# GLA level operands prepared two levels ahead, and background steps moved inside the seven-product units

## The chip, the cores and the metric

One NeuronCore of a Trainium2 chip runs the whole program in one launch. The metric is the device time of one execution in microseconds (us). Five engines matter: TensorE (PE) does matmuls, VectorE (DVE) and ScalarE (ACT) do elementwise work and empty the matmul banks (PSUM), GpSimd (POOL) does a little elementwise work and issues some transfers, and SyncE (SP) issues most of the transfers. Each engine works through its own instruction list in order.

## The reference

One decoder layer of width 1024 over 512 tokens, all in float32. After a layer norm, one input projection feeds gated linear attention (GLA, 4 heads), latent attention (MLA, 8 heads) and the gates; the two branches are gated and projected out; a second layer norm and a squared-ReLU MLP of hidden width 4096 follow.

```python
q_g, k_g, v_g, r_g, a_lr, q_lat, kv_lat, gate_logits = split(h @ w_in)
log_a = log_sigmoid(a_lr @ w_gla_a2 + b_gla_a2) / 16
o_gla = gla(q_g, k_g, v_g, log_a)            # o_t = q_t S_t, S_t = diag(a_t) S_{t-1} + k_t^T v_t
y_gla = (rms_norm(o_gla) * silu(r_g)) @ w_o_gla
y_mla = merge_heads(mla(q_lat, kv_lat)) @ w_o_mla
h = layer_norm(ALPHA * h + (g_gla * y_gla + g_mla * y_mla) @ w_out)
out = layer_norm(ALPHA * h + square(relu(h @ w_ff1)) @ w_ff2)
```

## The kernel before, in words

**Weights.** A weight strip of 512 KB is loaded into a buffer `wraw` (three buffers; SP queue, line 176). ACT copies its rounded part to `whi` (line 191), DVE the remainder to `wlo` (line 192), two buffers each. Every product is then three matmuls: high by high, and the two cross terms. Three places (the output-gate projection `proj_r`, the branch gates `g0` and `g1`, the first MLP matrix `f1`) use a scheme with seven block products instead of eight; in `proj_r` some summed weights and in `g0`/`g1` also the summed activations (`sh`) come from DRAM. The summed weights of a gate unit are made by loading one block into a buffer `wq` from SP (line 1181) and adding a second block to it by an accumulating transfer issued from POOL (line 1183).

**GLA by levels.** `gla_levels(h)` computes, for one head, the 512x512 causal score matrix by halving: for spans s = 1, 2, 4, ... 256 it fills the blocks in which a query and a key are in neighbouring spans of length s. The operand `qk` holds query and key of the head and is scaled in place from level to level. One level consists of

- `update(s)` (line 804, DVE): multiply `qk` in place by the decays of level s;
- `pack(2s)` (line 812, two ACT instructions; line 809 for s = 128): copy the rows that the next level needs into a buffer `M`;
- two matmuls on `M` into a bank `px` (line 864; line 867 for s = 128; line 871 takes s = 256 straight from `qk`);
- `take` (line 817, two DVE instructions): copy the wanted elements of that bank into the score buffer `SD`.

Because the scaling is in place, `pack(2s)` needs `update(s)`, and the next update needs `pack(2s)` to have read.

**What sets the order.** The program is written as one main sequence of matrix products, beside which background routines (Python generators) are stepped: `lane_levels` runs `gla_levels` for heads 0 to 3, `lane_out` the outputs `gla_out` of each head (lines 914 to 936), `r_out` the evictions of `proj_r`, `h_load` the loads of `sh`. `tick(n)` steps the first n routines once, `finish` and `levels_upto` step some until they end. A scheduler that simulates the program turns this into one fixed instruction list for each engine, so the places of the ticks and the order of the statements in a generator change the lists, and nothing is decided at run time. Main sequence around the change: values of heads 0 and 1 (`proj_v(0)`, lines 281 to 283), `proj_r` (lines 752 to 754), values of heads 2 and 3 (`proj_v(1)`, lines 247 to 283 are the general products), then the gate units `g0` and `g1` (lines 1208 to 1210), with the rest of the GLA in between.

**Names.** In the lists, `px_1914` or `M_1901` is one allocation; line numbers shift a little in the changed kernel: 804, 809, 812 and 817 become 803, 808, 811 and 816; 850 stays; 864 to 936 and 1181 to 1233 become higher by two; 1249 becomes 1250.

Of the kernel before, what the change touches and what calls it, by code (L numbers as in the profile page):

```python
# [52 lines left out]
def tile_hybrid_block(ctx: ExitStack, tc: tile.TileContext, I, out, dbg=None):  # L53
# [36 lines left out]
    def PX(shape=(P, T), dt=F32, n="px"):  # L90
        return px.tile(list(shape), dt, tag="px", name=nm(n))
# [132 lines left out]
    def tick(width):  # L224
        for g in list(active[:width or WID[0]]):
            step(g)
# [79 lines left out]
    PL["k"] = plan("w_in", C_K, T)  # L306
    WQ = {}

    RY, RA4 = (4, 4, 2, 2, 1, 2, 2), "t1"
    RW = (("11", 0), ("21", 1), ("t2", 3), ("t1", 2), ("t3", 6), ("22", 5), ("t4", 4))  # L310

    def r_src(op, hf):
# [394 lines left out]
    def proj_r():  # L707
        bank, e, xs = {}, {}, {}

        def x_load(ph):  # L710
            xs[ph] = []
            for p in range(4):
                t = B([P, 2, 256], F32R, "xr")
                x = (2, 3, 5, 6).index(ph)
                nc.sync.dma_start(f(t), hsd[p][x // 2][:, x % 2])
                xs[ph].append((t[:, 0], t[:, 1]))

        def r_out(ph, bank, e):
            for t in range(2):
                a, b = bank["a", t], bank["b", t]  # L720
                if ph == 4:
                    silu(0, 2 + t, a)
                else:
                    o, x, y, op, j, tt = {1: (0, b, e.get((0, t)), ALU.add, 0, t), 6: (2, e.get((2, t)), a, ALU.subtract, 1, 2 + t),
                                          5: (3, b, e.get((3, t)), ALU.subtract, 1, t)}[ph]
                    vtt(e[o, t], x, y, op=op)
                    yield
                    silu(j, tt, e[o, t])
                yield

        nat = {0: (0, 0), 1: (1, 0), 4: (1, 1)}
        for n, (op, ph) in enumerate(RW):
            if n + 1 < len(RW) and RW[n + 1][1] not in nat:
                x_load(RW[n + 1][1])
            if ph in nat:
                i, h = nat[ph]
                x = [tuple(hT[2 * p + i][:, w, 256 * h:256 * h + 256] for w in range(2)) for p in range(4)]
            else:
                x = xs.pop(ph)
            opens = ph in (0, 1, 2)  # L740
            for hf in range(2):
                it = PL["r"][2 * n + hf]
                pump(it)
                hi, lo = stream[it]["w"]
                for pp in range(2):
                    xh, xl = x[2 * hf + pp]
                    for t in range(2):
                        key = ("a" if ph in (0, 3, 6, 4) else "b", t)
                        if ph in (0, 1) and not hf and not pp:
                            bank[key] = MM()  # L750
                        o, c = bank[key], slice(t * P, (t + 1) * P)
                        mm(o, xh[:, c], hi[:, pp], start=opens and not hf and not pp, stop=False, skip_group_check=True)  # L752
                        mm(o, xh[:, c], lo[:, pp], start=False, stop=False, skip_group_check=True)
                        mm(o, xl[:, c], hi[:, pp], start=False, stop=hf == 1 and pp == 1, skip_group_check=True)
                    if (hf, pp) != (1, 1):
                        tick(None)
            if ph in (0, 3, 2):
                for t in range(2):
                    e[ph, t] = B([P, T], F32, "er")
                    act(e[ph, t], bank["b" if ph == 2 else "a", t], AF.Copy)  # L760
            else:
                spawn(r_out(ph, bank, e))
                if ph in (4,):
                    finish(active[-1])
            tick(None)

            if op == RA4:
                r_acc4()
# [22 lines left out]
    def gla_levels(h):  # L791
# [10 lines left out]
        def update(s):  # L802
            v = lr(qk, s)
            vtt(v, v, view(D, off[s] + 1, (2, T // (2 * s)), (-1, 2), (0, s)), op=ALU.mult)

        def pack(s):
            M = B([P, T], F32, "M")
            if s == 128:
                act(M.rearrange("p (n two s) -> p n two s", two=2, s=s), lr(qk, s), AF.Copy)
            else:  # L810
                for i, w in enumerate((T + 256 + s, T + s - 256)):
                    act(pairs(M[:, i * 256:(i + 1) * 256], s), view(k0, i * 256, (2 * s, 128 // s), (w, 2), (1, s)), AF.Copy)
            return M

# [26 lines left out]
        vtt(v, v, view(D, 1, (2, T // 2), (-1, 2)), op=ALU.mult)  # L841
        v = view(k0, T + 1, (2, T // 2))
        vtt(v, v, D[:, T:T + T // 2], op=ALU.mult)
        yield
        px1 = []
        for i in range(2):
# [2 lines left out]
                c = (2 * i + t) * P  # L849
                mm(p[:, t * 192:(t + 1) * 192], x0[:, c:c + P], xs[i][:, t, :], start=True, stop=True)  # L850
            px1.append(p)
        M = pack(2)
        yield
        for i, p in enumerate(px1):
            pt = p[:, :384].rearrange("p (t c) -> p t c", c=192)
# [3 lines left out]
        prev, s = None, 2  # L859
        while s < T:  # L860
            p = PX()
            if s <= 64:
                for i in range(2):
                    mm(p[:, i * P:(i + 1) * P], M[:, i * P:(i + 1) * P], M[:, 256 + i * P:256 + (i + 1) * P], start=True, stop=True)
            elif s == 128:
                for i in range(2):
                    mm(p[:, i * P:(i + 1) * P], M[:, 2 * i * P:(2 * i + 1) * P],
                       M[:, (2 * i + 1) * P:(2 * i + 2) * P], start=True, stop=True)
            else:
                for j in range(2):  # L870
                    mm(p[:, j * 256:(j + 1) * 256], qk[:, 0, j * P:(j + 1) * P], qk[:, 1, 256:], start=True, stop=True)
            if prev is not None:
                take(*prev)
            prev = (s, p)
            if s < 256:
                update(s)
            s *= 2
            if s < 256:
                M = pack(s)
            if s == 16 and h + 1 < GH:  # L880
                decays(h + 1)
            yield
# [302 lines left out]
    def unit(key, ops, evac, after=None, pb=None):  # L1185

        bank, e1, e5, u2 = {}, {}, {}, {}

        def prod(op):
            ph = dict(FMO)[op]  # L1190
            opens = ph in (0, 2, 1)
            for g in range(UNITS[key][2]):
                bk = ("a" if ph in (0, 3, 6, 4) else "b" if ph in (2, 5) else "c", g)
                if ph == 1 and key == "g0":
                    bank[bk] = bank["b", g]
                elif opens:
                    bank[bk] = (PX if ph == 1 else (pb or MM) if ph == 2 else MM)()
                o, it = bank[bk], PL[key, op, g]
                pump(it)
                hi, lo = stream[it]["w"]  # L1200
                for k in range(4):
                    while len(ops) <= k or ph not in ops[k]:
                        tick(3)
                    xh, xl = ops[k][ph]
                    for a in range(2):
                        c = slice(a * P, (a + 1) * P)
                        oa = o[:, a * 256:(a + 1) * 256]
                        mm(oa, hi[:, k, c], xh, start=opens and k == 0 and a == 0, stop=False, skip_group_check=True)  # L1208
                        mm(oa, hi[:, k, c], xl, start=False, stop=False, skip_group_check=True)  # L1209
                        mm(oa, lo[:, k, c], xh, start=False, stop=k == 3, skip_group_check=True)  # L1210
                    if k == 1:
                        tick(3)
                if ph == 0:
                    e1[g] = B([P, T], F32, "e1")
                    act(e1[g], o, AF.Copy)
                elif ph == 1:
                    vtt(e1[g], o, e1[g], op=ALU.add)
                    evac(0, 0, g, e1[g], True)
                elif ph == 2:
                    e5[g] = B([P, T], F32, "e5")  # L1220
                    act(e5[g], o, AF.Copy)
                elif ph == 3:
                    u2[g] = B([P, T], F32, "u2")
                    act(u2[g], o, AF.Copy)
                if ph == (5 if key == "g0" else 3):
                    vtt(u2[g], bank["b", g], u2[g], op=ALU.subtract)
                    evac(1, 0, g, u2[g], True)
                if ph == 6:
                    vtt(e5[g], e5[g], o, op=ALU.subtract)
                    evac(1, 1, g, e5[g], True)  # L1230
                elif ph == 4:
                    evac(0, 1, g, o, False)
                tick(3)
            if after:
                after(op)
        return prod
# [101 lines left out]
    t1, mv = mla_pair(1)  # L1338
# [345 lines left out]
```

## Time and profile before

| | |
|---|---|
| median of 3 executions | 882.56 us (882.06 to 883.23) |
| the profiled execution | 882.95 us |
| its span, first to last instruction | 881.1 us |
| PE busy, and its share of the span | 859.6 us, 98% |
| mean granted PE clock | 0.996 |
| DVE, ACT, POOL busy | 72%, 53%, 16% |

All times below are counted from the start of the span, and the 1.85 us between span and execution time lie outside it. A row of a timeline gives start, length, engine, source line, operation and tiles, then in brackets how long the engine was idle before it and what it had waited for. Matmuls overlap: a 128x256 matmul of 0.28 us is followed by the next after 0.12 us. A windows row gives, for a stretch of the span, the busy time of each engine with its instruction count, the granted PE clock (1.00 is full), the busy share of the 16 transfer engines (it passes 1 where packets overlap) and the rate.

### The profile page before, as it was taken

The page shows a single profiled execution, that of the slowest core. Times are in us where ns is not written, and L with a number is a line of the kernel's source. Part 1 is how long each engine was busy: PE and PEld are TensorE (multiplying, and loading weights), DVE is VectorE, ACT ScalarE, POOL GpSimd, SP SyncE. Part 2 cuts the span into 40 slices and gives each one's busy share as a digit, 9 for nine tenths or more (in the row PEclk, how much of TensorE's full clock was granted, in tenths as well). Part 3 has the DMA queues.
Part 4 walks back from the last instruction along what each step waited for, and adds up shares of the span by engine and source line. Part 5 has one row for each costly group of instructions (what it writes and reads, how often), then busy time and mean ns, then how long its engine had stood idle before and what let it go on. Part 6 is the DMA issues. An engine that isn't in the chain of part 4 may idle for free.

```text
span 881.1 us, 12813 instructions
## 1 busy us (share of the span) xinstructions
PE 859.6 (98%) x4765; PEld 750.3 (85%) x4765; DVE 634.4 (72%) x1037; ACT 469.0 (53%) x821; POOL 144.6 (16%) x184
## 2 busy tenths in 40 slices
PE   5999999999999999999999999999999999999996
PEld 5988888889989978888888888988888888889985
DVE  7959988877655646656766798886567646788865
ACT  5556767654565624435554414566357446656820
POOL 0323305030101030300000003004400520141000
PEclk9999999999999999999999999999999999999999
DMA  7995945595828443321207527007931990499312
GB/s 240 282 232 146 332 145 121 191 267 198 197 70 197 141 130 102 102 66 58 93 26 270 183 84 275 1 0 192 281 101 40 270 240 25 89 236 227 119 63 79
DMA packets 95213, 134.57 MB, mean 153 GB/s; under 512 B 12672, under 2 KB 58112, under 8 KB 95152
## 3 DMA queue, kind: packets, MB, share of 16 engines
q1 hardware_dynamic: 73840, 92.36, 33.3%
q0 software_dynamic: 19392, 37.76, 19.8%
q10 hardware_dynamic: 1920, 3.66, 1.1%
q8 instruction: 37, 0.61, 0.3%
q14 instruction: 24, 0.20, 0.1%
HBM read 110.15 MB, written 8.91 MB: 135 GB/s over the span
## 4 chain that ended last, share of the span: by engine, by line
PE 94%; DVE 2%; ACT 2%; DMA 1%; issue 0%; POOLq 0%; SPq 0%; DVEq 0%; ACTq 0%
PE mm L247 11%; PE mm L248 11%; PE mm L249 11%; PE mm L283 5%; PE mm L281 5%; PE mm L282 5%; PE mm L1208 4%; PE mm L1210 4%; PE mm L1209 4%; PE px L1496 2%; PE px L1495 2%; PE px L1497 2%; PE mm L1496 2%; PE mm L1495 2%; PE mm L1497 2%; PE mm L752 1%
## 5 line engine op out<-in xcount | busy, mean ns | idle before, releaser
L192 DVE TENSOR_TENSOR wlo<-wraw,whi 128x1024 fp32r<-128x1024 f32 (+1 forms) x90 | 99.3, 1104 | 92.1 <-ACT whi L191 85.7
L191 ACT ACTIVATE whi<-wraw 128x1024 fp32r<-128x1024 f32 (+1 forms) x90 | 85.6, 951 | 91.3 <-PE mm L248 43.4
L248 PE MATMUL mm<-h,whi 128*128 128x512 f32 x224 | 87.2, 389 | 0.0
L247 PE MATMUL mm<-h,whi 128*128 128x512 f32 x224 | 87.1, 390 | 0.0
L249 PE MATMUL mm<-h,wlo 128*128 128x512 f32 x224 | 83.2, 390 | 0.0
L192 DVE TENSOR_TENSOR wlo<-wq,whi 128x1024 fp32r<-128x1024 f32 x44 | 54.0, 1226 | 32.2 <-ACT whi L191 32.2
L1514 POOL DMA_DIRECT2D res<-ev x42 | 37.7, 1035 | 184.3 <-ACT ev L1512 150.5
L191 ACT ACTIVATE whi<-wq 128x1024 fp32r<-128x1024 f32 x44 | 46.5, 1058 | 34.7 <-PE mm L1209 22.2
L1210 PE MATMUL mm<-sh,wlo 128*128 128x256 f32 x176 | 50.0, 284 | 0.0
L1209 PE MATMUL mm<-sh,whi 128*128 128x256 f32 x176 | 49.8, 283 | 0.0
L1208 PE MATMUL mm<-sh,whi 128*128 128x256 f32 x176 | 49.8, 283 | 0.0
L249 PEld LDWEIGHTS mm<-h,wlo 128*128 128x128 f32 x224 | 42.0, 188 | 9.1 <-DVE wlo L192 0.4
L247 PEld LDWEIGHTS mm<-h,whi 128*128 128x128 f32 x224 | 42.1, 188 | 8.7
L248 PEld LDWEIGHTS mm<-h,whi 128*128 128x128 f32 x224 | 42.0, 188 | 8.7
L191 ACT ACTIVATE xh<-wraw 128x1024 fp32r<-128x1024 f32 (+1 forms) x28 | 27.2, 987 | 28.0 <-PE mm L283 15.6
L192 DVE TENSOR_TENSOR xl<-wraw,xh 128x1024 fp32r<-128x1024 f32 (+1 forms) x28 | 31.3, 1131 | 9.0 <-ACT xh L191 9.0
L1557 ACT ACTIVATE relu<-mm 128x512 f32<-128x512 f32 x24 | 14.1, 596 | 42.0 <-PE mm L249 42.0
L1208 PEld LDWEIGHTS mm<-sh,whi 128*128 128x128 f32 x176 | 33.8, 192 | 0.0
L1209 PEld LDWEIGHTS mm<-sh,whi 128*128 128x128 f32 x176 | 33.8, 192 | 0.0
L1210 PEld LDWEIGHTS mm<-sh,wlo 128*128 128x128 f32 x176 | 33.8, 192 | 0.0
L1208 PE MATMUL mm<-h,whi 128*128 128x256 f32 x112 | 31.9, 285 | 1.2 <-ACT whi L191 1.2
L1210 PE MATMUL mm<-h,wlo 128*128 128x256 f32 x112 | 32.0, 285 | 0.7 <-DVE wlo L192 0.7
(481 smaller groups left out, 2704.3 us busy)
## 6 DMA issues: line engine op xcount, KB each, us to landing
wraw<-in_w_ff_dram SPq DMA_DIRECT2D x36, 512.0 KB, 5.1
wraw<-in_w_in_dram SPq DMA_DIRECT2D x30, 512.0 KB, 4.5
wq<-in_w_ff_dram POOLq DMA_DIRECT2D x26, 512.0 KB, 8.9
res<-ev POOLq DMA_DIRECT2D x42, 256.0 KB, 9.8
wq<-in_w_in_dram SPq DMA_DIRECT2D x20, 512.0 KB, 6.3
wq<-in_w_in_dram POOLq DMA_DIRECT2D x18, 512.0 KB, 9.7
hsd<-hs SPq DMA_DIRECT2D x16, 256.0 KB, 4.4
xr<-hsd SPq DMA_DIRECT2D x16, 256.0 KB, 4.2
```

What stands on the lines that cost most here:

```text
L191: st["ins"] = act(hi[:, :nk, :n], raw[:, :nk, :n], AF.Copy)
L192: st["lo"] = vtt(lo[:, :nk, :n], raw[:, :nk, :n], f(hi[:, :nk, :n]), op=ALU.subtract)
L247: mm(o, hi[:, c], xh, start=first, stop=False)
L248: mm(o, hi[:, c], xl, start=False, stop=False)
L249: mm(o, lo[:, c], xh, start=False, stop=last)
L281: mm(o, xh, hi[:, :n], start=opens, stop=False, skip_group_check=share)
L282: mm(o, xh, lo[:, :n], start=False, stop=False, skip_group_check=share)
L283: mm(o, xl, hi[:, :n], start=False, stop=last, skip_group_check=share)
L1208: mm(oa, hi[:, k, c], xh, start=opens and k == 0 and a == 0, stop=False, skip_group_check=True)
L1209: mm(oa, hi[:, k, c], xl, start=False, stop=False, skip_group_check=True)
L1210: mm(oa, lo[:, k, c], xh, start=False, stop=k == 3, skip_group_check=True)
L1514: nc.gpsimd.dma_start(res[tt + t][:, j * T:(j + 1) * T], e, accum_op=ALU.add)
```

## The change

Three edits.

1. In `gla_levels`, the operands are made two levels ahead of their product. `pack(2)` comes before the first yield, `update(2)` and `pack(4)` right after the first products; in the loop, after the product of level s come `update(2s)` and `pack(4s)`, and only then `take` of the level before. The same operations are done, with one more `M` buffer alive.
2. In `proj_r`, the ticks move from behind a slice (both token halves) to between its two halves, at three of the four slices of a product; the tick after the eviction goes. That is 21 ticks for 28.
3. In `unit`, the two ticks of a product stand in its first and third slice, not in the second and after the eviction.

```diff
-    RY, RA4 = (4, 4, 2, 2, 1, 2, 2), "t1"
+    RY, RT, RA4 = (4, 4, 2, 2, 1, 2, 2), ((0, 0), (1, 0), (1, 1)), "t1"
...
                         mm(o, xl[:, c], hi[:, pp], start=False, stop=hf == 1 and pp == 1, skip_group_check=True)
-                    if (hf, pp) != (1, 1):
-                        tick(None)
+                        if t == 0 and (hf, pp) in RT:
+                            tick(None)
...
                 if ph in (4,):
                     finish(active[-1])
-            tick(None)
...
+        Ms = [pack(2)]
         yield
         px1 = []
...
             px1.append(p)
-        M = pack(2)
+        update(2)
+        Ms.append(pack(4))
         yield
...
             p = PX()
+            M = Ms.pop(0) if s < 256 else None
             if s <= 64:
...
+            if s <= 64:
+                update(2 * s)
+            if s <= 32:
+                Ms.append(pack(4 * s))
             if prev is not None:
                 take(*prev)
             prev = (s, p)
-            if s < 256:
-                update(s)
             s *= 2
-            if s < 256:
-                M = pack(s)
...
-                    if k == 1:
+                    if k % 2 == 0:
                         tick(3)
...
                 elif ph == 4:
                     evac(0, 1, g, o, False)
-                tick(3)
```

The number of instructions is the same on every engine (PE has 4685 matmuls in both). PE's list differs only from the values of heads 0 and 1 up to the end of the first gate products, apart from two neighbouring transposes that change places far later; the lists of the other engines differ in the same stretch. Three places show what moves.

**PE, last GLA head (head 3), in `proj_v(1)`.** `M` is the packed operand of a level, `px` the bank of its product; lines 914 to 916 (916 to 918 in the changed kernel) are output products of another head, lines 281 to 283 products of `proj_v(1)`. Before, the products of levels 4, 8 and 16:

```order
L283 MATMUL mm_2013<-whi_2005,h_21_140 128x512
L864 MATMUL px_1914<-M_1901 128x128 x2
L864 MATMUL px_1936<-M_1920 128x128 x2
L864 MATMUL px_1963<-M_1942 128x128 x2
L914 MATMUL px_1973<-vh_1341,sd_1367 128x256
L915 MATMUL px_1973<-vl_1342,sd_1367 128x256
L916 MATMUL px_1973<-vh_1341,sd_1367 128x256
L864 MATMUL px_2021<-M_1969 128x128 x2
L914 MATMUL px_2030<-vh_1341,s_281_1370 128x256
```

Now, the products of levels 2, 4 and 8 and what follows:

```order
L282 MATMUL mm_1961<-wlo_2008,h_27_156 128x512
L866 MATMUL px_2051<-M_1984 128x128 x2
L866 MATMUL px_2070<-M_2021 128x128 x2
L283 MATMUL mm_1961<-whi_2007,h_27_156 128x512
L866 MATMUL px_2100<-M_2055 128x128 x2
L936 MATMUL px_2109<-ca,og_2079 128x128 x2
L936 MATMUL px_2109<-ca,og_2080 128x128 x2
L281 MATMUL mm_1921<-whi_2090,h_30_164 128x512
```

Three level products of this head still stand close together. But between the head's first products (line 850) and its first level product lie 38 rows of other work now, where 2 rows lay between them before; and the later levels are spread over the following strips. In the same way head 1's last three products on `M` (lines 864, 864, 867), which stood in three consecutive rows of PE's list before, now have three 512-wide products of `proj_r` between each two.

**ACT, end of unit `g0`.** `whi` is the split of the next weight strip, `osq` squares of GLA outputs, `gt` gates, `u` an eviction; before, the strip `whi_2763` (last block, first half) is placed ahead of the eviction `u_2625`, and PE's list has that block's products ahead of those of block t3, second half (`whi_2729`):

```order
L191 ACTIVATE whi_2729<-wq_2000 128x1024
L918 ACTIVATE osq_2583,gss_2570<-px_2571 128x256
L191 ACTIVATE whi_2763<-wq_2431 128x1024
L918 ACTIVATE osq_2611,gss_2570<-px_2601 128x256
L1249 ACTIVATE gt_2673<-e_521_2479,hbg 128x256
L1249 ACTIVATE gt_2675<-e_521_2479,hbg 128x256
L1224 ACTIVATE u_544_2625<-mm_2361 128x512
```

Now:

```order
L191 ACTIVATE whi_2721<-wq_1912 128x1024
L920 ACTIVATE osq_2593,gss_2580<-px_2581 128x256
L920 ACTIVATE osq_2617,gss_2580<-px_2607 128x256
L1226 ACTIVATE u_544_2625<-mm_2353 128x512
L1250 ACTIVATE gt_2717<-u_544_2625,hbg 128x256
L1250 ACTIVATE gt_2719<-u_544_2625,hbg 128x256
L191 ACTIVATE whi_2763<-wq_2419 128x1024
L1250 ACTIVATE gt_2673<-e_521_2479,hbg 128x256
L1250 ACTIVATE gt_2675<-e_521_2479,hbg 128x256
L920 ACTIVATE osq_2649,gss_2580<-px_2607 128x256
L191 ACTIVATE whi_2796<-wq_2421 128x1024
```

The eviction `u` moved ahead of the next strip, and PE takes the blocks in the order in which they are written: t3 first half, t3 second half, then the last block's two halves.

**SP, loads for `proj_v(1)` and `g0`.** `wraw` are the strips of `proj_v(1)`, `wq` the blocks for `g0`. Before, the four strips stand ahead of the six blocks:

```order
L176 DMA wraw_1885<-in_w_in_dram 128x2x512
L176 DMA wraw_1924<-in_w_in_dram 128x2x512
L176 DMA wraw_2003<-in_w_in_dram 128x2x512
L176 DMA wraw_2080<-in_w_in_dram 128x2x512
L1181 DMA wq_1987<-in_w_in_dram 128x4x256
L1181 DMA wq_1990<-in_w_in_dram 128x4x256
L1181 DMA wq_1993<-in_w_in_dram 128x4x256
L1181 DMA wq_1995<-in_w_in_dram 128x4x256
L1181 DMA wq_1997<-in_w_in_dram 128x4x256
L1181 DMA wq_2000<-in_w_in_dram 128x4x256
```

Now:

```order
L176 DMA wraw_1832<-in_w_in_dram 128x2x512
L1183 DMA wq_1899<-in_w_in_dram 128x4x256
L1183 DMA wq_1902<-in_w_in_dram 128x4x256
L176 DMA wraw_1857<-in_w_in_dram 128x2x512
L1183 DMA wq_1905<-in_w_in_dram 128x4x256
L1183 DMA wq_1907<-in_w_in_dram 128x4x256
L1183 DMA wq_1909<-in_w_in_dram 128x4x256
L1183 DMA wq_1912<-in_w_in_dram 128x4x256
L176 DMA wraw_1915<-in_w_in_dram 128x2x512
L176 DMA wraw_2005<-in_w_in_dram 128x2x512
```

The second strip of `proj_v(1)` now stands behind two of `g0`'s blocks, the third and the fourth behind all six.

## The prediction

> **What bounds the kernel now.** The page comes first. Its chain, followed back from the last instruction, is almost all matmul work, so only time in which PE stands still, or runs slowly, is to be had:
>
> ```profile
> PE 94%; DVE 2%; ACT 2%; DMA 1%; issue 0%; POOLq 0%; SPq 0%; DVEq 0%; ACTq 0%
> ```
>
> Next the waits view for PE alone (total us, times, longest). Besides the start of the program, four kinds of wait matter, and all lie where the change moves instructions:
>
> ```profile
> PE px L864 <- ACT M L812: 2.0, 2, 1.0
> PE mm L1208 <- ACT whi L191: 1.2, 1, 1.2
> PE px L867 <- ACT M L809: 0.8, 1, 0.8
> PE mm L1210 <- DVE wlo L192: 0.7, 1, 0.7
> ```
>
> The windows view, cut at these waits, shows that nothing else between 97 and 300 us is idle: the four stretches below hold all of the missing 203.00 - 198.37 = 4.63 us. The second also has a lower clock.
>
> ```profile
> 143.00:146.00 3.00, 2.25 (x14) 1.84 (x14) 3.00 (x8) 2.72 (x6) 0.00 (x0) 1.00 0.91 248
> ...
> 181.00:189.00 8.00, 6.03 (x36) 5.58 (x35) 5.81 (x18) 3.23 (x10) 2.07 (x2) 0.79 1.17 256
> ...
> 246.00:249.00 3.00, 1.79 (x14) 1.51 (x13) 1.84 (x2) 2.60 (x8) 0.00 (x0) 1.00 0.00 0
> ...
> 256.00:258.00 2.00, 1.31 (x11) 1.10 (x10) 2.00 (x3) 1.97 (x4) 0.00 (x0) 1.00 0.00 0
> ...
> sum 203.00, PE 198.37 PEld 181.98 DVE 152.56 ACT 122.12 POOL 32.92; mean PE 22.04 PEld 20.22 DVE 16.95 ACT 13.57 POOL 3.66
> ```
>
> **What one wait costs.** It is more than its idle time: the row before it, otherwise overlapped by its follower, runs out alone, and the row after it is longer. PE's timeline at the longest wait:
>
> ```profile
> 246.26 0.28 PE L1209 MATMUL mm<-sh,whi 128*128 128x256 f32 x1
> 246.38 0.28 PE L1210 MATMUL mm<-sh,wlo 128*128 128x256 f32 x1
> 247.87 0.38 PE L1208 MATMUL mm<-h,whi 128*128 128x256 f32 x1 [1.21 <-ACT whi L191]
> 248.09 0.28 PE L1209 MATMUL mm<-h,whi 128*128 128x256 f32 x1
> ```
>
> The usual start-to-start is 0.12 us. Here 246.38 to 247.87 is 1.49, and 247.87 to 248.09 is 0.22: lost 1.37 + 0.10 = 1.47 us for 1.21 us of idle, so 0.26 us on top of each wait.
>
> **Term 1, head 1 at 144 us.** Three level products stand in a row on PE; the last needs a pack that ACT reaches late:
>
> ```profile
> 140.58 0.63 ACT L788 ACTIVATE dec<-gs 128x508 f32<-128x508 f32 x1 [1.30 <-POOL gs L786]
> ...
> 143.62 0.61 ACT L809 ACTIVATE M<-qk 128x512 f32<-128x512 f32 x1
> ```
>
> In the new ACT list this pack follows `dec` at once, since the level's update no longer waits for a product to be taken. So it is ready at about 141.2 + 0.6 = 141.8; counting PE's new list with the row spacings of before, the product comes at 142.9. Gain 0.75 + 0.26 = 1.0 us, margin about 1 us. The one `M` more that is alive I put at nothing: it comes from a pool of 22 buffers, whose return no row here is waiting for; if a pack had to wait for one, that would take the margin and cost up to one pack, 0.6 us.
>
> **Term 2, head 3 at 181 to 185 us.** PE's waits, and ACT's packs for the successive levels:
>
> ```profile
> 182.74 0.71 PE L864 MATMUL px<-M 128*128 128x128 f32 x4 [0.95 <-ACT M L812]
> ...
> 184.84 1.22 PE L864 MATMUL px<-M 128*128 128x128 f32 x4 [1.03 <-ACT M L812]
> ```
>
> ```profile
> 178.31 0.73 ACT L812 ACTIVATE M<-qk 128x256 f32<-128x256 f32 x2 [1.87 <-DVE qk L804]
> ...
> 180.15 0.73 ACT L812 ACTIVATE M<-qk 128x256 f32<-128x256 f32 x2 [0.58 <-DVE qk L804]
> 181.96 0.72 ACT L812 ACTIVATE M<-qk 128x256 f32<-128x256 f32 x2 [1.09 <-DVE qk L804]
> ...
> 184.07 0.72 ACT L812 ACTIVATE M<-qk 128x256 f32<-128x256 f32 x2
> ```
>
> A level comes each 1.81 to 2.11 us, and PE asks for several in a row. The change does not shorten the step from update to pack, for scaling in place keeps them serial; it starts the steps earlier relative to the products. Three packs now need about 2 x 1.84 + 0.73 = 4.4 us from the first, while PE has 38 rows, by my count 8.6 us, between the head's first products and its first product on `M`. Even with the two operands' splits in between, some 3 us are left. Gain 0.95 + 1.03 + 2 x 0.26 = 2.5 us. DVE is the queue on which the wait could return: the update stands behind og and split work there, and the packs, and behind them on ACT the next strip's split, would be late with it.
>
> **Term 3, the clock.** Right after these two waits:
>
> ```profile
> 184.90:188.30 3.40, 3.40 (x16) 0.51 1.18 238
> ```
>
> ```profile
> 181.40:184.80 3.40, 1.47 (x11) 1.06 (x9) 3.40 (x12) 2.84 (x8) 0.77 (x1) 1.00 1.16 266
> 244.60:248.00 3.40, 2.19 (x19) 1.98 (x18) 1.54 (x3) 1.60 (x5) 0.00 (x0) 1.00 0.00 0
> ```
>
> For 3.40 us PE ran at 0.51: 3.40 x 0.49 = 1.67 us lost. The 3.40 us before held 1.47 us of work, 43%; around the longest single wait 64% was left and no drop followed. I take it that a drop needs something between, so it goes with term 2.
>
> [...]
>
> **Term 4, the gate unit at 246 and 256 us.** ACT and then DVE:
>
> ```profile
> 246.40 0.39 ACT L918 ACTIVATE osq<-px 128x256 f32<-128x256 f32 x1 [2.36 <-PE px L916]
> ...
> 246.77 1.05 ACT L191 ACTIVATE whi<-wq 128x1024 fp32r<-128x1024 f32 x1
> ```
>
> ```profile
> 255.99 1.23 DVE L192 TENSOR_TENSOR wlo<-wq,whi 128x1024 fp32r<-128x1024 f32 x1
> ```
>
> At 246 the split of the last block waited behind an `osq` that needs PE; at 256 the `wlo` of its second half ended at 257.22, and PE went on at 257.27. PE's new list has the t3 blocks in their natural order: a strip's buffer is free when the first t3 product ends, 24 matmuls x 0.12 = 2.9 us before the next strip is needed, and the split takes 1.05 + 1.23 = 2.3 us. Gain 1.47 + 0.69 + 0.26 = 2.4 us, with a margin of only 0.6 us for the `wlo` of each strip.
>
> **The sum.** 1.0 + 2.5 + 1.67 + 2.4 = 7.6 us: 882.95 - 7.6 = 875.35 against the profiled execution, if nothing returns. Of the three tight places (head 1's pack, two `wlo`) I let two come back at the smallest size, 0.69 + 0.26 = 0.95 each: 877.25. The profiled run lies 0.39 us above the median, so 876.9. Bounds: none back gives 875.0; two back and the clock with them 878.5. The fewer ticks of `proj_r` cost no instruction; they could only make head 3 late, which is the next rival.
>
> **Rivals.**
>
> *A wait at head 3 stays.* Three of its products still stand almost in a row. If PE meets the chain there, two waits of today's size and the clock return, 2.5 + 1.67 = 4.2: 882.95 - 7.6 + 4.2 - 0.39 = 879.2. Against it: the 8.6 us of other work.
>
> *The waits only move* (the change does not do what it says). The step per level is unchanged, and elsewhere (head 0's products on `M` also stand three in a row now) as much could be lost as is won: 882.95 - 0.39 = 882.6, with 881 as its lower end. For it: 1.8 us per level on ACT and DVE. Against it: PE now has the longer stretches of work between levels.
>
> [...]
>
> *Slower: strips late behind `g0`'s blocks.* SP now issues all six blocks ahead of the third strip of `proj_v(1)`, where the strips went first before; the accumulating transfers share the engines with them.
>
> ```profile
> 177.00:182.00 5.00, 4.79 (x29) 4.08 (x27) 5.00 (x14) 2.02 (x6) 2.59 (x2) 1.00 1.10 354
> 183.00:190.00 7.00, 5.97 (x32) 5.56 (x32) 3.81 (x12) 3.19 (x12) 2.57 (x2) 0.76 1.17 238
> ```
>
> ```profile
> q1 hardware_dynamic: 830, 0.83, 43.7%
> ```
>
> ```profile
> 172.20 5.19 SPq L1181 DMA_DIRECT2D wq<-in_w_in_dram  x6
> 177.48 17.32 SPq L176 DMA_DIRECT2D wraw<-in_w_in_dram  x2
> ```
>
> ```profile
> 192.09 1.06 ACT L191 ACTIVATE whi<-wraw 128x1024 fp32r<-128x1024 f32 x1 [0.64 <-DMA wraw<-in_w_in_dram]
> ```
>
> Loads alone move 354 GB/s; beside accumulates SP's queue gets 0.83 MB in 7 us, 119 GB/s, and one strip, issued at 177.48 behind the six blocks, landed at 192.0, 14.5 us later. In the new lists the third strip can be issued at about 168 (its buffer is free at 163, six blocks take 5 us to issue), so by that row it lands near 182.7; PE needs its split at 187.3, so it must land by 186.2. If it lands at 193 instead, PE waits 6.8 + 0.26 us and the clock halves for two stretches, 3.34: 10.4 us, 875.35 + 10.4 - 0.39 = 885.4. From a landing at 190.2 on the whole gain is gone. Against it: a margin of 3.5 us by the worst transfer seen.
>
> **How the numbers follow.** Forecast 62%, a wait left at head 3 12%, clock alone 4%, waits moved 15%, late strips 7%. The time is the forecast's, 876.9. From 874.8 to 882.6 leaves out the late strips, half of the moved waits and a little below: about 18%. The three executions lie 1.17 us apart, so a measurement can tell about 0.2%, 1.8 us, from no change. The first three cases are faster by more, 0.78; the moved waits mostly within, 0.14; slower 0.08.
>
> **What would show it.** Right: the waits view of PE loses the rows for 866, 869, 1210 and 1212, or keeps them at half the size; windows around head 3 show PE full and the clock at 1.00; ACT's packs of head 3 end microseconds before PE's products. Wrong: a wait of PE on `M` of over 1 us anywhere between 100 and 210 us, a clock under 0.9 in any stretch but the last, ACT `whi` waiting on the transfer of `wraw` between 175 and 200 us, or SP's strips landing later than 186 us.

## The result, and the profile after

| | before | changed |
|---|---|---|
| median of 4 executions | 882.89 us | 876.16 us (875.22 to 876.66) |
| ratio, 95% interval | | 0.9922 [0.9905, 0.9939] |
| profiled execution, its span | 882.95, 881.1 us | 876.66, 874.4 us |
| PE idle between 97 and 300 us (profiled) | 4.63 us | 0 |

The median before is 882.89 us with a fourth execution; the three known at the prediction gave 882.56.

The waits view of PE in the changed kernel, in the same columns (total us, times, longest): of the four kinds of wait none is left, and one on `wlo` has come up that was not there.

```profile
PE px L446 <- ACT x L435: 8.4, 1, 8.4
PE px L1212 <- DVE wlo L192: 0.7, 1, 0.7
PE px L446 <- DVE lnt L453: 0.3, 1, 0.3
PE mm L247 <- ACT h L449: 0.3, 1, 0.3
PE mm L247 <- DVE rt L976: 0.2, 1, 0.2
```

The same windows as before show PE full in all four stretches, and the clock at 1.00 (before: 2.25, 6.03, 1.79 and 1.31 us busy, the second at 0.79):

```profile
143.00:146.00 3.00, 3.00 (x17) 2.59 (x16) 3.00 (x9) 2.87 (x7) 0.43 (x1) 1.00 0.59 108
...
181.00:189.00 8.00, 8.00 (x45) 6.94 (x44) 3.69 (x6) 3.35 (x10) 2.11 (x2) 1.00 1.14 297
...
246.00:249.00 3.00, 3.00 (x27) 3.00 (x27) 2.97 (x6) 1.93 (x4) 0.00 (x0) 1.00 0.00 0
...
256.00:258.00 2.00, 2.00 (x19) 2.00 (x19) 1.23 (x1) 1.01 (x2) 1.07 (x1) 1.00 1.09 354
...
sum 203.00, PE 203.00 PEld 187.52 DVE 155.00 ACT 128.71 POOL 32.11; mean PE 22.56 PEld 20.84 DVE 17.22 ACT 14.30 POOL 3.57
```

Matching PE's rows of the two profiles one by one accounts for the whole difference. Where the lists agree again, the distance between a row and its partner shows what was won so far: the changed kernel is 0.15 us late at 95 us and 7.56 us early at 258 us: 7.71 us come from the stretch that the change touches. At 788 us the new wait gives 0.81 back, which leaves 6.7 us of span. The time outside the span is 2.26 us, where it was 1.85, so the profiled executions differ by 6.3 us.

Head 3 in the changed kernel, on ACT. A strip's split waits 3.62 us for its transfer, and then come the packs of the levels:

```profile
184.52 1.06 ACT L191 ACTIVATE whi<-wraw 128x1024 fp32r<-128x1024 f32 x1 [3.62 <-DMA wraw<-in_w_in_dram]
185.48 0.77 ACT L811 ACTIVATE M<-qk 128x256 f32<-128x256 f32 x2
...
187.47 0.72 ACT L811 ACTIVATE M<-qk 128x256 f32<-128x256 f32 x2 [0.85 <-DVE qk L803]
...
188.95 0.73 ACT L811 ACTIVATE M<-qk 128x256 f32<-128x256 f32 x2
...
190.85 0.73 ACT L811 ACTIVATE M<-qk 128x256 f32<-128x256 f32 x2 [0.23 <-DVE qk L803]
```

And on PE, the strip's first use and the head's first products on `M`:

```profile
188.43 0.40 PE L281 MATMUL mm<-whi,h 128*128 128x512 f32 x1
188.67 0.39 PE L282 MATMUL mm<-wlo,h 128*128 128x512 f32 x1
```

```profile
193.67 1.05 PE L866 MATMUL px<-M 128*128 128x128 f32 x8
194.48 0.48 PE L283 MATMUL mm<-whi,h 128*128 128x512 f32 x1
194.79 0.60 PE L866 MATMUL px<-M 128*128 128x128 f32 x4
```

A level still takes 1.5 to 2.0 us (185.48, 187.47, 188.95, 190.85), but the third pack ends at 189.68 and its product comes at 194.79: the packs are 5 to 7 us ahead. The strip's rounded part `whi` is ready on ACT at 185.58, 2.85 us ahead of its use at 188.43. The remainder `wlo` comes later, from DVE:

```profile
185.61 1.23 DVE L192 TENSOR_TENSOR wlo<-wraw,whi 128x1024 fp32r<-128x1024 f32 x1 [3.52 <-ACT whi L191]
```

It ends at 186.84 and is needed at 188.67, so the strip's margin is the smaller one, 1.8 us.

### The profile page after: what moved, and what is told of

Read it like the earlier page. It is cut to its first block, busy times and chain, and to the rows that moved or that the text cites. A ratio compares the mean times of both kernels' runs of the same rounds, so it can differ in the third digit from the quotient of the medians.

```text
span 874.4 us, 12828 instructions
## 1 busy us (share of the span) xinstructions
PE 857.4 (98%) x4765; PEld 748.0 (86%) x4765; DVE 633.8 (72%) x1037; ACT 469.4 (54%) x821; POOL 143.8 (16%) x184
## 4 chain that ended last, share of the span: by engine, by line
PE 91%; DVE 4%; DMA 3%; issue 1%; ACT 1%; SPq 0%; POOLq 0%; DVEq 0%; POOL 0%; ACTq 0%
PE mm L247 11%; PE mm L248 11%; PE mm L249 11%; PE mm L283 5%; PE mm L281 5%; PE mm L282 5%; PE mm L1212 4%; PE mm L1210 4%; PE mm L1211 4%; PE px L1496 2%; PE px L1497 2%; PE px L1498 2%; PE mm L754 1%; PE mm L753 1%; PE mm L752 1%; DMA res<-ev 1%
```

## The experiments

Each run is compared with the kernel before on the same chip; the median of that was 881.93, 881.93 and 882.3 us on the three chips. The last column is PE's idle time in us between 97 and 300 us in the run's profile. Line numbers differ by a few lines from run to run.

| run | edits in it | median | ratio, 95% interval | idle |
|---|---|---|---|---|
| e1 | GLA | 880.14 | 0.9977 [0.9968, 0.9986] | 2.78 |
| e2 | ticks of `proj_r` | 880.77 | 0.9988 [0.9977, 0.9998] | 3.44 |
| e3 | ticks of `unit` | 884.83 | 1.0032 [1.0020, 1.0045] | 6.67 |
| e4 | both ticks | 876.53 | 0.9940 [0.9927, 0.9954] | 1.08 |
| e10 | GLA, `proj_r` | 879.38 | 0.9967 [0.9957, 0.9977] | 2.36 |
| e5 | all (the change) | 875.17 | 0.9916 [0.9901, 0.9930] | 0.21 |
| e6 | all, 21 ticks at the old place | 875.84 | 0.9921 [0.9906, 0.9935] | 0 |
| e7 | all, 28 ticks inside | 879.96 | 0.9976 [0.9965, 0.9987] | 3.62 |
| e8 | both ticks, `take` last | 876.89 | 0.9932 [0.9918, 0.9947] | 1.08 |
| e9 | all, one strip loaded twice | 883.17 | 1.0007 [0.9999, 1.0016] | 4.96 |

**One edit at a time.** Theory A is the prediction's: packs started earlier (the GLA edit) remove the waits of heads 1 and 3 and with them the half clock, the ticks of `unit` those of the gate unit. Theory B: what counts is how far apart PE's level products stand, and this is set by the ticks of `proj_r`.

e1 has the `gla_levels` part of the diff alone, e2 the `proj_r` part, e3 the `unit` part, e4 the last two; nothing else is edited.

> The kernel before with only the GLA edit (operands two levels ahead). Theory A, the prediction's: packs that start earlier remove the waits at head 1 and head 3 and the half clock, 1.0 + 2.5 + 1.7 = 5.2 us, and the two waits in the gate unit (2.4) stay: about 877.7 against 882.9. Theory B, spacing: what counts is how far apart PE's level products stand, and that is set by the ticks in proj_r; in this list head 1's products are spread but three of head 3's still stand in a row, 10 matmuls after its second product, so only head 1's 1.0 us goes: about 881.9, with the waits on M at head 3 and the stretch at half clock still there.

```profile
PE mm L1211 <- ACT whi L191: 1.2, 1, 1.2
PE mm L1213 <- DVE wlo L192: 0.7, 1, 0.7
PE px L867 <- DVE SD L817: 0.4, 1, 0.4
...
PE px L867 <- ACT M L812: 0.3, 1, 0.3
```

The waits view of e1: head 1's wait is gone, head 3 keeps 0.7 of 2.0 us, and the gate unit's two waits stand at their old size. 1.8 us were won: nearer to B (1.0) than to A (5.2), but more than B allowed at head 3.

> The kernel before with only the ticks of proj_r moved between the token halves (21 for 28). Theory A: without earlier packs nothing is won, 882.9, the waits on M move but stay over 1 us each. Theory B: head 3's levels come 108 matmuls after head 2's and the three of head 1 stand 12 and 9 matmuls apart, so the waits on M and the half clock go without any change in gla_levels: 5.2 us, about 877.7, with the gate unit's waits (2.4 us) left, since its blocks still stand out of order.

```profile
PE mm L1209 <- DVE wlo L192: 2.0, 2, 1.3
PE px L1209 <- DVE wlo L192: 1.8, 1, 1.8
PE px L866 <- ACT M L808: 1.1, 1, 1.1
...
PE mm L1207 <- ACT whi L191: 0.3, 1, 0.3
```

The waits view of e2: both waits that stood at 144 and at 182 to 185 us are gone without any change in `gla_levels`, as B has it. But a wait of 1.1 us has come up on the last pack (s = 128, at 205 us), the gate unit waits 2.4 us, and the first MLP unit 1.8 us on `wlo`. So only 1.2 us were won.

> The kernel before with only the ticks of the seven-product units moved into their first and third slice. Both theories: the waits of the gate unit at 246 and 256 us go, 2.4 us, about 880.5; the waits on M at 144 and 181 to 185 us and the half clock stay as before. If the gate unit's waits stay, they were not due to these ticks but to the lateness that head 3 hands on.

```profile
PE mm L1210 <- DVE wlo L192: 2.6, 2, 2.0
PE px L864 <- ACT M L812: 2.0, 2, 1.0
PE mm L1208 <- ACT u L1224: 1.3, 1, 1.3
PE px L867 <- ACT M L809: 0.8, 1, 0.8
PE px L1210 <- DVE wlo L192: 0.7, 1, 0.7
```

Both theories missed. The waits of the levels stay, as expected, but the gate unit's grow from 1.90 to 3.92 us, and the kernel is 2.9 us slower than before.

> Both tick edits, without the GLA edit. Theory A: only the gate unit's 2.4 us, about 880.5. Theory B: all four kinds of waits go, 7.6 us, 875.3, or about 876.1 if a wait of 0.7 us comes up later as in the changed kernel; then the GLA edit adds nothing that can be measured.

```profile
PE px L866 <- ACT M L808: 1.1, 1, 1.1
PE px L446 <- DVE lnt L453: 0.5, 1, 0.5
```

Here all of the gate unit's waits are gone; only the one at 205 us is left. A falls: most of the gain (5.4 us; all three edits gain 6.8 in e5) comes without the GLA edit.

**What the unit ticks are worth.** e10 has the GLA and the `proj_r` part, not the `unit` part.

> GLA edit and proj_r ticks, without the unit ticks. If the unit ticks are worth something only once head 3 is moved: no wait on M, and in the gate unit the three waits that the proj_r ticks alone left (0.3, 0.8, 1.3 us idle and 0.26 more each, 3.1 us): about 879. If the unit ticks are worth nothing at all: 875.8.

```profile
PE mm L1212 <- DVE wlo L192: 2.0, 2, 1.3
...
PE mm L1210 <- ACT whi L191: 0.3, 1, 0.3
```

879.38, as expected: no wait on `M`, and in the gate unit the three waits that e2 has, to the hundredth (0.31, 0.76, 1.29 us). So once head 3 has been moved the unit ticks win 4.2 us (e2 to e4, on one chip; about 1.8 of it is a wait in the first MLP unit that only e2's profile shows), and without that they lose 2.9. The products of the gate unit are free of waits only in the runs that have the unit ticks and 21 ticks in `proj_r` (the changed kernel, e4, e5, e6, e8, e9). Which place in the lists makes the two edits need each other was not isolated. The GLA edit with the unit ticks alone was not run; e7 below is the nearest to it.

**Number or place of the ticks in proj_r.**

```diff
-                        if t == 0 and (hf, pp) in RT:
-                            tick(None)
+                    if (hf, pp) != (1, 1):
+                        tick(None)
```

That is e6: the ticks at their old place, the one after the eviction still left out. e7 instead adds a fourth tick inside:

```diff
-    ... RT, RA4 = ..., ((0, 0), (1, 0), (1, 1)), "t1"
+    ... RT, RA4 = ..., ((0, 0), (0, 1), (1, 0), (1, 1)), "t1"
```

> The changed kernel once more, beside the next three. Expected 876.2, no wait on M and none in the gate unit; if the wait of 0.7 us on wlo at 788 us (first MLP unit, where all lists are unchanged) is a matter of when transfers land, it is there with another size or not at all.

> The changed kernel, but the three ticks of a product of proj_r stand behind a slice again; only the tick after the eviction stays away (21 ticks). If the number of ticks counts, which leaves head 3 for proj_v(1): 876.2, as the changed kernel. If the place between the halves counts: a wait on M of over 1 us comes back, 878 to 880.

> The changed kernel with ticks between the halves of all four slices (28 ticks, as many as before). If the number counts: head 3's levels fall into the start of proj_v(1) again, three of its products in a row, waits on M of 0.7 us in all as with the GLA edit alone, perhaps the gate unit's 2.4 us too: 877.5 to 880. If the place counts: 876.2.

The waits view of e7:

```profile
PE mm L1210 <- ACT whi L191: 1.2, 1, 1.2
PE px L866 <- ACT M L811: 0.9, 2, 0.6
PE mm L1212 <- DVE wlo L192: 0.7, 1, 0.7
PE mm L752 <- DMA xr<-hsd: 0.6, 1, 0.6
PE px L1212 <- DVE wlo L192: 0.5, 1, 0.5
```

The number counts. With 21 ticks at the old place the kernel is the changed one within 0.7 us (e6 875.84, e5 875.17, intervals overlapping); with 28 inside, level waits and both gate waits (1.2 and 0.7, the sizes of before) are back and 4.8 us of the gain are lost. With a step less in each product of `proj_r`, head 3 falls into the middle of `proj_v(1)`: in e2's list of PE, 108 matmuls stand between head 2's last product on `M` and head 3's first. The traces show the same in the other runs: between head 3's first products and its first product on `M`, PE has 2 rows of other work in the kernel before, in e1, e3 and e7, 36 in e2, e4 and e8, and 38 in e5, e6, e10 and the changed kernel.

**What of the GLA edit is needed.** e8 has both tick edits, and in `gla_levels` only `take` moved behind update and pack; the operands are made one level ahead, as before:

```diff
-            if prev is not None:
-                take(*prev)
-            prev = (s, p)
             if s < 256:
                 update(s)
-            s *= 2
-            if s < 256:
-                M = pack(s)
+            if s < 128:
+                M = pack(2 * s)
+            if prev is not None:
+                take(*prev)
+            prev = (s, p)
+            s *= 2
```

> Both tick edits, and of the GLA edit only that take comes after update and pack; operands one level ahead, not two. With both tick edits alone a wait of 1.1 us on the last pack (s = 128) was left at 205 us. If the place of take on DVE makes it, it goes here: 875.3 to 876.2. If two levels of lead are needed, it stays at about 1 us: 876.5.

ACT in e8 shows that the wait of 1.1 us stayed, and why:

```profile
204.94 0.38 ACT L917 ACTIVATE osq<-px 128x256 f32<-128x256 f32 x1 [0.24 <-PE px L915]
...
205.31 0.62 ACT L808 ACTIVATE M<-qk 128x512 f32<-128x512 f32 x1
```

The last pack stands behind an `osq` that waits for PE, and PE then waits for the pack. With two levels of lead this pack ran at 198.86 in the changed kernel, 5 us before that stretch. So the second level of lead is needed, for this one wait of 1.08 + 0.26 us.

**The rival of late strips.** e9 is the changed kernel with the third strip of `proj_v(1)` loaded twice:

```diff
+                    if e.get("twice"):
+                        nc.sync.dma_start(dst, src)
...
+    stream[PL["v", 1]["idx"][2]]["twice"] = True
```

> The changed kernel with the third weight strip of proj_v(1) loaded twice into the same buffer, so that its split has to wait for the second load (work added, nothing left out). In the changed kernel that strip landed at 184.4 us and PE took it at 188.4. Rival of late strips: beside the accumulating transfers (119 GB/s) the second load lands at 190 to 194; PE waits 3 to 6 us, and the clock halves for a stretch of 3.4 us after it: 880 to 884. If strips are not what the place hangs on (order of products hides it): 876 to 877. On the clock: if the drop belongs to a fixed grid of 3.41 us windows, it comes only if one of these is idle by more than about half.

```profile
193.10 2.00 ACT L193 ACTIVATE whi<-wraw 128x1024 fp32r<-128x1024 f32 x2 [4.08 <-DMA wraw<-in_w_in_dram]
```

```profile
185.45:188.87 3.42, 2.67 (x19) 2.26 (x17) 1.23 (x5) 0.94 (x4) 0.18 (x1) 1.00 1.20 234
188.87:192.28 3.41, 1.13 (x8) 0.97 (x8) 2.25 (x7) 0.14 (x1) 0.86 (x1) 1.00 1.14 235
192.28:195.69 3.41, 1.48 (x4) 1.21 (x5) 1.50 (x2) 2.59 (x4) 0.00 (x0) 0.50 0.07 12
195.69:199.10 3.41, 3.41 (x13) 2.93 (x12) 3.05 (x8) 1.36 (x4) 0.00 (x0) 0.50 0.70 188
```

The scheduler knows of the second load, so the lists differ too: 15 rows of other work stand between head 3's first products and its first product on `M`, not 38, and that product comes ahead of the late strip's. The split starts at 193.1, PE stands still for 1.0 and 4.0 us, and the clock is halved for two stretches of 3.41 us: 883.17, all of the gain gone. A late strip is a real danger, as the rival said; the change stays clear of it by 1.8 us.

**The clock.** e11 and e12 are one more profile each of the kernel before, unchanged:

> The kernel before, one more profile. Its two waits at head 3 will be there. If the clock is ruled by a fixed grid of 3.41 us windows, it halves only if one window holds nearly both waits (idle by over half): time 883 to 884 then, 881 to 882 otherwise. If 43% of work in any 3.4 us is enough, as the prediction took it, it halves in every execution.

> As the run before it: the same kernel at another phase of the grid, if there is one.

Times were 881.44 and 881.22. The waits are the same as in the first profile, yet in e11 no half clock follows, and e12 took 0.22 us less than e11. In e11, a stretch of 3.40 us around both waits of head 3 holds even less work, 1.41 us, than the 1.47 us of the first profile, and the clock stays at 1.00 in it and after it, to 189.07 us in the windows below:

```profile
181.50:184.90 3.40, 1.41 (x12) 1.01 (x10) 3.40 (x12) 2.88 (x8) 0.43 (x1) 1.00 1.17 261
```

So the prediction's reading, that 43% of work in any 3.4 us is enough, falls. In the first profile the clock changed at 184.84 and 188.25 us and, at its end, at 877.75; from the first to the last of these are 203.0 steps of 3.413 us, the length of the stretch at half clock. That the clock changes only at such steps is an estimate from these three times. In windows cut at these steps (the grid that the expectations speak of), the first profile of before shows one with 1.44 us of work, then one at half clock:

```profile
181.43:184.84 3.41, 1.44 (x11) 1.03 (x10) 3.41 (x12) 2.88 (x8) 0.81 (x1) 1.00 1.16 264
184.84:188.25 3.41, 3.41 (x16) 3.41 (x17) 1.97 (x6) 0.31 (x2) 0.52 (x2) 0.50 1.17 238
```

In e11, cut at its own steps (counted back from the clock's last change), the same two waits are shared between two windows:

```profile
178.84:182.25 3.41, 3.00 (x18) 2.41 (x16) 3.41 (x11) 1.72 (x5) 1.28 (x1) 1.00 1.10 347
182.25:185.66 3.41, 1.83 (x13) 1.63 (x14) 3.41 (x12) 2.96 (x9) 1.19 (x1) 1.00 1.18 238
185.66:189.07 3.41, 3.41 (x23) 3.08 (x22) 1.67 (x5) 1.45 (x6) 0.54 (x2) 1.00 1.17 238
```

Cut so, a window idle for 58% (before), 67% (e9) or 56% (e2, at its end, 871.87 to 875.28 us) was followed by half clock, and so was one idle for 57% that itself ran at half clock (e9). Windows idle for 48% (e3) and 46% (e11) were not. In e12 the windows idle for 22 and 36%, to 185.17 us, ran at 1.00. The two whose idle shares are closest, from e3 (the next window had the clock at 1.00) and from e2 (the next at 0.50; the run's mean clock was 0.997):

```profile
182.05:185.46 3.41, 1.79 (x13) 1.59 (x14) 3.41 (x12) 3.00 (x9) 1.11 (x1) 1.00 1.18 238
```

```profile
871.87:875.28 3.41, 1.50 (x13) 1.29 (x11) 2.66 (x7) 0.00 (x0) 0.81 (x1) 1.00 0.00 0
```

In these six windows the clock went with the idle share of a window cut so; that it does beyond them was not shown. The times fit: of 23 executions of before on the last chip, twelve took 881.1 to 882.3 us with a mean clock of 0.997 to 0.999, eleven 882.65 to 884.2 with 0.996. Only the first profile shows an execution of the slower group window by window, so that each of them holds such a drop is likely, not shown.

## Why the prediction was right, and where it was not

The time was 876.16 us, forecast 876.9; the profiled execution took 876.66, where the sum gave 877.25. That they lie so close is in part luck: of the 1.9 us let come back only 0.81 came, at a place that was not named, and 0.41 came from the time outside the span.

- **Where the gain lies, and its size.** Right. All of it comes from the stretch of the waits: 7.71 us, against a sum of 7.6 from 4.63 us of idle time, 0.26 for each of five waits, and the clock. This holds for the profiled pair; what the clock adds in other executions is term 3.
- **Term 1, head 1.** Right: the pack follows `dec` and ends at 141.55 (forecast 141.8), the product comes at 143.44 (142.9). Either the GLA edit or the `proj_r` ticks alone is enough.
- **Term 2, head 3.** The size was right, the reason only in part. "It starts the steps earlier relative to the products" is, alone, worth 1.25 of the 1.99 us of idle (e1). The 38 rows of other work come from `proj_r`'s ticks (2 rows without them in e1, 36 with them alone in e2), of which the prediction said only that they cost nothing and could make head 3 late. They make it late, and that is the gain.
- **Term 3, the clock.** This is the step that was wrong. "I take it that a drop needs something between, so it goes with term 2": the same two waits come without a drop (e3, e11, and by its time e12). By the estimate from the windows above, it hung on how the waits fell into the steps of 3.41 us: 1.44 us of work in one window in the first profile, 3.00 and 1.83 us in two in e11. The profiled execution of before was one of the slower ones. In a median the term is worth less than its 1.67 us: on e5's chip the executions of before with a mean clock of 0.997 or more have the median 881.33, and the others 883.87. Against the former the change (875.17) wins 6.2 us, against the latter 8.7. The case "clock alone" did not come true: the changed kernel has no drop before 870.03 us, after its last matmul.
- **Term 4, the gate unit.** The waits are gone, but not because of its own ticks alone, which make it worse (e3). The prediction did not name the other condition, the place of head 3: without the unit ticks 2.36 us of idle time are left (e10), without the later head 3 3.92 (e3). Why both are needed stays open.
- **Two waits let come back, 1.9 us.** None of the three named places did. One came at 788 us, in a part with unchanged lists, 0.74 us of idle. It was 0.54 us in e12, which is the kernel before, 1.82 in e2, 0.47 to 0.76 in e3, e5, e7 and e8, and absent in the other runs, e6 and e11 among them. That it goes with the arrival of transfers is likely but was not tested.
- **Rivals.** Late strips was the nearest: the third strip landed about 184.4 (forecast 182.7) with 1.8 us to spare, and landing at 193 costs about 8 us (e9 against e5 on another chip, 883.17 to 875.17) where 10.4 was worked out for an unchanged list. PE's list in e9 had work to place ahead of the late strip, until 190.2, and part of the first slow stretch was idle anyway: 4.96 us of idle time, 2 x 0.26, and half of the 1.48 and 3.41 us of work in the two slow stretches make 7.9.

## What to carry to other kernels

Where a static list is made from stepped routines, the number of steps in one phase decides into which later phase the rest falls; try it before rewriting the routine, and try edits together, since one that loses alone can win in the place that another makes. Prepare an operand so early that its place in the list is ahead of any instruction that waits for the engine which needs it: a pack behind an `osq` that waits for PE made PE wait 1.08 us in turn (e8). Before a term of half clock from a single profile enters a sum, take a second profile of the same kernel.

## What the runs showed of the hardware

In the kernel before, the granted clock of PE was 0.50 for 3.41 us, from 184.84 to 188.25 us. In the 3.41 us ahead of that PE had worked 1.44 us, with no single idle time above 1.03 us (0.95 and 1.03 us). The clock fell when both waits were over: the 1.67 us, worked out from that stretch, were paid for after them. In e11, the same kernel with the same waits, the clock was 1.00 from 178.84 to 189.07 us. The executions of this kernel with a mean clock of 0.996 or less and those with 0.997 or more have medians 1.5 to 2.5 us apart on the three chips. In the kernel before, loads alone moved 354 GB/s (177 to 182 us); beside accumulating transfers their queue moved 119 GB/s (0.83 MB from 183 to 190 us), and 118 in the changed kernel (0.94 MB from 173 to 181 us).
